# The last four of 32 inner tiles of an MLP's second product as plain block products instead of seven-product ones

## The chip, the cores and the metric

The kernel runs on one core of one Trainium2 chip. The metric is the device time of one execution in microseconds (us); the figure for a kernel is the median of its runs. Five engines work side by side in a core, each on its own list of instructions in a fixed order: TensorE (PE, matmuls), VectorE (DVE), ScalarE (ACT), GpSimd (POOL) and SyncE (SP, which here only issues DMA transfers). An engine waits where an instruction needs something that another engine or a transfer has not yet delivered, or a buffer that is not yet free. SBUF is the on-chip memory of 128 partitions, PSUM the small memory into which matmuls accumulate.

## What is computed

The reference is a decoder layer with a mixing part, cross-attention and an MLP, on 1024 tokens of width 1024 in float32. Only its end matters here:

```python
hf = rmsnorm(x, norm_mlp[l])
x = x + jnp.square(jax.nn.relu(hf @ mlp_w1[l])) @ mlp_w2[l]
...
return rmsnorm(x, norm_final)
```

The hidden width is 4096. The first product (hf with mlp_w1) gives the hidden values, which are made non-negative and squared; the second product (with mlp_w2) sums over the 4096 hidden values, that is over 32 inner tiles of 128. Its result is added to x, and every row of 1024 values is then divided by its root mean square and multiplied by a gain.

## The kernel before

**Number format.** Every float32 operand of a matmul is split into a high and a low part: ACT writes the high part (`split`, L70, a cast), and DVE or POOL subtracts it from the source to get the low part (L71). A product is then three matmuls into the same PSUM tile: high by high, high by low, low by high (`mm3`, L59, L60, L61). A matmul is 128 x 128 by 128 x 512.

**Seven products in place of eight.** Both MLP products treat their operands as 2 x 2 blocks. `LEFT` and `RIGHT` (L1058 and L1059) name for each k from 1 to 7 the block, or the sum or difference of blocks, that stands on either side. The weight's sums S1 to S4 are formed by `left` (L1064 to L1071, four instructions on tiles); those of the other side are T1 to T4.

**First product** (`mlp1`, called by `mlp_in` for pairs p = 0 to 15, seven products each). A pair yields two tiles `hab`, each with two blocks: B11 and B12, B21 and B22, made non-negative and squared on the way (`emit`, L1149 to L1155). When all four blocks of a pair are there, four subtractions on DVE (L1160 to L1163) form T1, T2, T3 and T4, and four DMA writes (L1165 to L1167) put the seven tiles of the names in `H1` (L1062) into the DRAM buffer `h1`: 512 KB each for the two `hab` and for `ht`, 256 KB for T4. Two neighbouring pairs, p = 2c and p = 2c + 1, fill `h1[c]`.

**Second product** (`mlp2`, called by `mlp_out` for passes c = 0 to 7). Pass c takes four of the 32 inner tiles. `w2_raw` loads 2 MB of weights (L1171) into one buffer of the pool `slotA` (four buffers, which the hidden units share) and calls `left` on POOL (L1066 to L1070). For each of the seven products `w2_unit` splits the weight operand (ACT L70, then L71 on POOL, in pass 7 on DVE for four of the seven) into a buffer of `wpool` (four buffers), and `h1_unit` loads the hidden operand (512 KB, L1188) through a buffer of `stage` (three buffers) and splits it (ACT L70, DVE L71). Weight loads and hidden loads are issued by SP in the program's order (`after("wdma", ...)`). Then four tiles st = 0 to 3 follow: six matmuls into one PSUM tile of the pool `m2` (six buffers), and one DVE instruction that adds the PSUM tile to the accumulator `acc[k]` for this product (`add`, L1199). So there are seven accumulators of 128 x 4 x 512 in SBUF; x itself is loaded into those of k = 2, 4, 5 and 3 in pass 0 (L1210), where the accumulators of k = 1, 6 and 7 are written by ACT.

**The last pass.** In pass 7 the seven accumulators are also put together, with `add` on tiles of 128 x 512: after a tile of product 1 comes acc[6] += acc[1] on DVE and acc[2] += acc[1] on POOL, and so on, each as soon as its product's tile is there. Four of the sums then are the four blocks of the result: acc[2] and acc[4] make one tile of rows, acc[5] and acc[3] another. Products come in the order 1, 6, 7, 2, 4, 5, 3, so the four rows of acc[2] and acc[4] are complete with product 4 and the other four with product 3. `out_rows` ends a row: for its first half a square with sum on ACT (L1242) and a product with the gain on POOL (L1243); for its second half the other square (L1249), the sum of both (POOL, L1251), the reciprocal root (`rstd`, DVE L96 and POOL L97), and then the two halves of the output, one on ACT (L1253) and one on DVE (L1255), each with a DMA to the output.

**What sets the order.** The program is written in the order above, but a scheduler orders the instructions of every engine by what they depend on and by which buffers are free. Instructions that are independent of the work around them may therefore stand earlier on an engine than in the program's text. Buffers are released tile by tile.

## Time and profile before

| | before |
|---|---|
| median of 3 runs (lowest to highest) | 2452.02 us (2450.01 to 2455.37) |
| the profiled execution's own time | 2450.84 us |
| its span, first to last instruction | 2448.9 us |
| mean granted TensorE clock | 0.985 of full speed |
| instructions | 31204 |
| shares of the chain that ended last | PE 51%, DVE 20%, DMA 11%, issue 8%, POOL 5%, ACT 4% |

The profile is of one execution. Rows of its views name an engine, a source line, the operation and the program's names for output and inputs; "x4" behind a row counts instructions that stand together, and the brackets give the idle time of the engine just before it and what ended that. Names say which buffers are meant: `wu` and `hu` are the split weight and hidden operands, `w` the loaded weights, `sth` the loaded hidden tile, `s` a sum of weight blocks, `ps` a PSUM tile, `acc` an accumulator, `xsf`, `ssf` and `rsf` the tiles of an output row, `hab` and `ht` the blocks of the first product.

### The profile page before, as it was taken

How to read it: one execution, taken by the hardware profiler on the slowest of the kernel's cores; microseconds unless marked ns; L12 is line 12 of the kernel's file. 1: busy time of each engine (PE TensorE's matmuls, PEld its weight loads, DVE VectorE, ACT ScalarE, POOL GpSimd, SP SyncE). 2: the span in 40 equal slices, each digit the busy share in tenths (PEclk: the TensorE clock that was granted, in tenths of full speed). 3: DMA queues.
4: the chain of work that ended last, by engine and by line, in shares of the span. 5: the costliest groups of instructions: out<-in, count | busy, mean ns of one | idle time of the engine just before them, and what ended most of it. 6: DMA issues, size and time to landing. Idle time of an engine off the chain costs nothing.

```text
span 2448.9 us, 31204 instructions
## 1 busy us (share of the span) xinstructions
PE 2312.1 (94%) x11132; PEld 1901.4 (78%) x11132; DVE 1885.1 (77%) x2920; ACT 1043.4 (43%) x1823; POOL 997.8 (41%) x644
## 2 busy tenths in 40 slices
PE   9999999999999989899998988999989999899996
PEld 7888878888887867677877766788768888778884
DVE  7677387877797787897787888345788888788888
ACT  5444355555555444545244444135432222343333
POOL 1122212221215434455422214034155555698787
PEclk9999999999999999999999989999999999999999
DMA  4222222222225345443576785343324443734431
GB/s 172 80 86 70 65 61 70 66 61 65 61 51 186 123 153 189 144 159 131 193 257 224 249 281 183 112 163 104 113 83 166 152 160 135 276 136 173 160 137 73
DMA packets 137258, 338.27 MB, mean 138 GB/s; under 512 B 17152, under 2 KB 27393, under 8 KB 137104
## 3 DMA queue, kind: packets, MB, share of 16 engines
q1 hardware_dynamic: 136528, 334.44, 41.5%
q8 instruction: 89, 1.46, 0.3%
q10 hardware_dynamic: 576, 1.84, 0.2%
q14 instruction: 65, 0.53, 0.1%
HBM read 229.21 MB, written 98.63 MB: 134 GB/s over the span
## 4 chain that ended last, share of the span: by engine, by line
PE 51%; DVE 20%; DMA 11%; issue 8%; POOL 5%; ACT 4%; SPq 0%; DVEq 0%; POOLq 0%; ACTq 0%
PE ps L61 7%; PE ps L59 7%; PE ps L60 7%; POOL wu L71 3%; PE psq L59 2%; PE psq L61 2%; PE psq L60 2%; PE sc L458 2%; PE psk L61 2%; DVE block L71 2%; PE psk L60 2%; PE psk L59 2%; DVE acc L1199 2%; DMA st<-oTs 1%; PE psv L60 1%
## 5 line engine op out<-in xcount | busy, mean ns | idle before, releaser
L59 PE MATMUL ps<-block,wu 128*128 128x512 f32 x1428 | 567.6, 398 | 48.3 <-DVE sf L1126 16.1
L61 PE MATMUL ps<-block,wu 128*128 128x512 f32 x1428 | 564.8, 396 | 22.3 <-DVE wu L71 15.2
L60 PE MATMUL ps<-block,wu 128*128 128x512 f32 x1428 | 560.7, 393 | 0.2 <-DVE block L71 0.2
L71 POOL TENSOR_TENSOR wu<-st,wu 128x512 fp32r<-128x512 f32 x144 | 226.0, 1577 | 385.4 <-ACT wu L70 341.8
L59 PEld LDWEIGHTS ps<-block,wu 128*128 128x128 f32 x1428 | 271.0, 190 | 111.9 <-ACT wu L70 29.0
L61 PEld LDWEIGHTS ps<-block,wu 128*128 128x128 f32 x1428 | 270.5, 189 | 90.5 <-DVE wu L71 18.6
L60 PEld LDWEIGHTS ps<-block,wu 128*128 128x128 f32 x1428 | 270.8, 190 | 60.0 <-DVE block L71 1.1
L70 ACT CAST wu<-st 128x512 fp32r<-128x512 f32 x240 | 141.3, 618 | 156.7 <-DVE st L1066 63.1
L59 PE MATMUL ps<-wu,hu 128*128 128x512 f32 x448 | 177.2, 395 | 16.9 <-DVE acc L1199 14.1
L71 POOL TENSOR_TENSOR w<-st,w 128x1024 fp32r<-128x1024 f32 x50 | 124.7, 2505 | 161.3 <-ACT w L70 161.3
L61 PE MATMUL ps<-wu,hu 128*128 128x512 f32 x448 | 174.7, 392 | 3.8 <-DVE hu L71 3.8
L60 PE MATMUL ps<-wu,hu 128*128 128x512 f32 x448 | 175.5, 392 | 0.0
L1199 DVE TENSOR_TENSOR acc<-acc,ps 128x512 f32<-128x512 f32 x216 | 137.8, 677 | 20.5 <-PE ps L61 20.0
L71 POOL TENSOR_TENSOR wu<-sf,wu 128x512 fp32r<-128x512 f32 x63 | 116.3, 1859 | 53.5 <-ACT wu L70 51.7
L71 DVE TENSOR_TENSOR hu<-sth,hu 128x1024 fp32r<-128x1024 f32 x56 | 121.1, 2167 | 20.4 <-ACT hu L70 19.9
L466 ACT ACTIVATE p<-sc,mx 128x256 f32<-128x256 f32 (+7 forms) x128 | 94.8, 741 | 69.9 <-DVE mx L463 50.2
L71 DVE TENSOR_TENSOR wu<-st,wu 128x512 fp32r<-128x512 f32 x96 | 90.1, 954 | 35.1 <-ACT wu L70 35.1
L59 PEld LDWEIGHTS ps<-wu,hu 128*128 128x128 f32 x448 | 84.6, 189 | 40.8 <-DVE acc L1199 12.2
L61 PEld LDWEIGHTS ps<-wu,hu 128*128 128x128 f32 x448 | 84.7, 189 | 22.9 <-DVE hu L71 5.1
L59 PE MATMUL psk<-block,w 128*128 128x512 f32 x256 | 102.2, 399 | 0.0
L61 PE MATMUL psk<-block,w 128*128 128x512 f32 x256 | 101.4, 396 | 0.0
L60 PE MATMUL psk<-block,w 128*128 128x512 f32 x256 | 101.3, 396 | 0.0
(389 smaller groups left out, 5638.5 us busy)
## 6 DMA issues: line engine op xcount, KB each, us to landing
sth<-h SPq DMA_DIRECT2D x56, 512.0 KB, 9.5
st<-in_w SPq DMA_DIRECT2D x32, 512.0 KB, 4.3
h<-hab SPq DMA_DIRECT2D x32, 512.0 KB, 2.8
w<-in_w SPq DMA_DIRECT2D x8, 2048.0 KB
sgb<-gsp SPq DMA_DIRECT2D x48, 256.0 KB, 4.6
gsp<-l SPq DMA_DIRECT2D x44, 256.0 KB, 4.0
acc<-y SPq DMA_DIRECT2D x40, 256.0 KB, 4.1
st<-in_w_br SPq DMA_DIRECT2D x18, 512.0 KB, 5.9
```

Of the source, the lines that this page charges most:

```text
L59: nc.tensor.matmul(ps, lhsT=lhs.hi, rhs=rhs.hi, start=start, stop=False)
L60: nc.tensor.matmul(ps, lhsT=lhs.hi, rhs=rhs.lo, start=False, stop=False)
L61: nc.tensor.matmul(ps, lhsT=lhs.lo, rhs=rhs.hi, start=False, stop=stop)
L70: ins = self.nc.scalar.copy(dst.hi, src)
L71: self.lo_ins = (lo_engine or self.nc.vector).tensor_tensor(dst.lo, src, f32(dst.hi), op=ALU.subtract)
L458: nc.tensor.matmul(sc[:, b * HB:b * HB + e], lhsT=qt[:, c, part, cols], rhs=k[b][:, c, 0:e], start=part == 0, stop=part == 1)
L466: nc.scalar.activation(p[:, 0:n], sc[:, 0:n], AF.Exp, bias=mx, accum_out=l)
L1199: eng.tensor_tensor(acc[k][:, st, :], acc[k][:, st, :], x if isinstance(x, bass.AP) else acc[x][:, st, :], op=ALU.add)
```

## The change

Pass 7 becomes a function of its own, `mlp2_last`, which computes the last four inner tiles as plain 2 x 2 block products: each of the four blocks of the result takes two products, eight in all, into the same PSUM tile (12 matmuls). No S or T is needed there, so `w2_raw` returns before `left` for c = 7, and `mlp1` ends for the last two pairs (p = 14 and 15) before the four subtractions and writes only the two `hab` tiles; `H1_LAST` names the four blocks that then lie in `h1[7]`. All eight operands, four weight blocks and four hidden blocks, are split ahead of the products; the weight blocks of the first half of the columns have their low parts on DVE, the others on POOL.

The seven accumulators are put together as they stand after pass 6: for each st seven additions on DVE (L1235). Then, for each st and each of its two rows, the two blocks of the row are computed and added to the accumulator (L1245), and the row is ended as before. A whole row is finished at a time, in eight steps.

```diff
+    H1_LAST = ("B11", "B12", "B21", "B22")
...
         if self.product(k, c, self.hf, self.p6(self.mps), v if p < 2 else nc.gpsimd, emit):
             a, b = c["h"]
+            dst = self.h1[p // 2][:, :, p % 2, :]
+            if p // 2 == 7:
+                for i, x in enumerate((a, b)):
+                    nc.sync.dma_start(dst[2 * i:2 * i + 2].rearrange("u p c -> p u c"), x)
+                return
             t, t4 = self.xw.tile([P, 2, HB], F32, tag="ts", name="ht", bufs=2), self.sraw[:, 6 + p % 2, :]
             tt(t[:, 0], a[:, 1], a[:, 0], ALU.subtract)
             tt(a[:, 1], b[:, 1], a[:, 1], ALU.subtract)
             tt(t[:, 1], b[:, 1], t[:, 0], ALU.subtract)
             tt(t4, b[:, 0], t[:, 1], ALU.subtract)
-            dst = self.h1[p // 2][:, :, p % 2, :]
             for i, x in enumerate((a, b, t)):
                 nc.sync.dma_start(dst[2 * i:2 * i + 2].rearrange("u p c -> p u c"), x)
             nc.sync.dma_start(dst[6], t4)
...
         t = self.slotA.tile([P, 4, D], F32, tag="s", name="w2")
         self.after("wdma", self.nc.sync.dma_start(t, self.a["w_2"][4 * c:4 * c + 4].rearrange("f p d -> p f d")))
         raw = {f"A{i + 1}{j + 1}": t[:, j::2, i * HB:(i + 1) * HB] for i in range(2) for j in range(2)}
+        if c == 7:
+            return raw
         self.left(raw, *(self.xw.tile([P, 2, HB], F32, tag=t, name="s2", bufs=2) for t in ("xt", "xt", "ts")), self.nc.gpsimd)
         return raw
...
         t = self.utile[:, self.n_units % 2]
         self.n_units += 1
         st = self.stage.tile([P, 2, HB], F32, tag="st", name="sth")
-        self.after("wdma", self.nc.sync.dma_start(st, self.h1[c, self.H1.index(name)]))
+        self.after("wdma", self.nc.sync.dma_start(st, self.h1[c, (self.H1_LAST if c == 7 else self.H1).index(name)]))
         u = Split(t[:, 0], t[:, 1])
         self.split(u, st)
         return u
-    def mlp2(self, c, acc, mps, gf):
+    def mlp2(self, c, acc, mps):
         nc, v, g = self.nc, self.nc.vector, self.nc.gpsimd
-        first, last = c == 0, c == 7
-        def add(k, x, st, eng=v):
-            eng.tensor_tensor(acc[k][:, st, :], acc[k][:, st, :], x if isinstance(x, bass.AP) else acc[x][:, st, :], op=ALU.add)
+        first = c == 0
         raw = self.w2_raw(c)
-        if last:
-            for st in range(4):
-                add(3, 5, st, g)
         for k in (1, 2, 4, 5, 7, 6, 3) if first else (1, 6, 7, 2, 4, 5, 3):
-            w, h = self.w2_unit(raw[self.LEFT[k]], v if last and k in (7, 4, 5, 3) else g), self.h1_unit(c, self.RIGHT[k])
+            w, h = self.w2_unit(raw[self.LEFT[k]], g), self.h1_unit(c, self.RIGHT[k])
             if first and k in (2, 4, 5):
                 x3 = self.x3.rearrange("(t s p) c -> s p t c", s=2, p=P)
                 for i, s, d in {2: ((2, 0, 0),), 4: ((4, 0, 1),), 5: ((5, 1, 1), (3, 1, 0))}[k]:
...
                 if first and k in (1, 6, 7):
                     nc.scalar.copy(acc[k][:, st, :], ps)
                 else:
-                    add(k, ps, st)
-                if not last:
-                    continue
-                if k == 1:
-                    add(6, 1, st)
-                    add(2, 1, st, g)
-                elif k == 6:
-                    add(7, 6, st)
-                    add(3, 6, st, g)
-                elif k == 7:
-                    add(4, 7, st)
-                    add(5, 7, st, g)
-                elif k == 5:
-                    add(3, ps, st)
-                self.out_rows(st, k, acc[k][:, st, :], gf)
...
+                    v.tensor_tensor(acc[k][:, st, :], acc[k][:, st, :], ps, op=ALU.add)
+    def mlp2_last(self, acc, mps, gf):
+        nc, v = self.nc, self.nc.vector
+        raw = self.w2_raw(7)
+        w, h = {}, {}
+        for k in range(2):
+            for x in ("A1", "A2"):
+                w[f"{x}{k + 1}"] = self.w2_unit(raw[f"{x}{k + 1}"], v if x == "A1" else nc.gpsimd)
+            h[f"B{k + 1}1"] = self.h1_unit(7, f"B{k + 1}1")
+        for k in range(2):
+            h[f"B{k + 1}2"] = self.h1_unit(7, f"B{k + 1}2")
+        for st in range(4):
+            for o, x in ((2, 1), (6, 1), (7, 6), (4, 7), (3, 6), (3, 5), (5, 7)):
+                v.tensor_tensor(acc[o][:, st, :], acc[o][:, st, :], acc[x][:, st, :], op=ALU.add)
+            for j in range(2):
+                xs = self.xw.tile([P, D], F32, tag=("ts", "xs")[j], name="xsf", bufs=2)
+                ss = self.small.tile([P, 2], F32, tag="ssf", name="ssf", bufs=8)
+                row = (2 * st + j + 4) % 8 * P
+                for i in range(2):
+                    ps = mps.tile([P, HB], F32, tag="m2", name="ps2")
+                    self.mmk(ps, [(h[f"B{k + 1}{j + 1}"][:, r, st * P:(st + 1) * P], w[f"A{i + 1}{k + 1}"][:, r, :])
+                                  for k in range(2) for r in range(2)])
+                    x = acc[2 + 2 * i + j][:, st, :]
+                    v.tensor_tensor(x, x, ps, op=ALU.add)
+                    sl = slice(i * HB, (i + 1) * HB)
+                    nc.scalar.activation(xs[:, sl], x, AF.Square, accum_out=ss[:, i:i + 1])
+                    if i == 0:
+                        nc.gpsimd.tensor_tensor(xs[:, sl], x, gf[:, sl], op=ALU.mult)
+                rs = self.small.tile([P, 1], F32, tag="rs", name="rsf", bufs=4)
+                nc.gpsimd.tensor_tensor(rs, ss[:, 0:1], ss[:, 1:2], op=ALU.add)
+                self.rstd(rs, rs, 1.0 / D, 1e-6)
+                nc.scalar.activation(xs[:, 0:HB], xs[:, 0:HB], AF.Copy, scale=rs)
+                nc.sync.dma_start(self.out[row:row + P, 0:HB], xs[:, 0:HB])
+                v.scalar_tensor_tensor(xs[:, HB:], x, rs, gf[:, HB:], op0=ALU.mult, op1=ALU.mult)
+                nc.sync.dma_start(self.out[row:row + P, HB:], xs[:, HB:])
...
             for i, k in enumerate(ks):
                 acc[k] = t[:, i]
         gf = self.gain(self.xw, 4)
-        for c in range(8):
-            self.mlp2(c, acc, mps, gf)
+        for c in range(7):
+            self.mlp2(c, acc, mps)
+        self.mlp2_last(acc, mps, gf)
     def run(self):
```

What takes the place of `out_rows` (L1235 to L1256 before, deleted) is in the last lines of `mlp2_last`; its steps on ACT, POOL and DVE are the same.

Three places show how instructions move in the lists of the engines.

The first is DVE in pass 6 and 7. Of the change, these rows stand where pass 6's products 6 and 7 are added up (`acc_18412` is the buffer of the accumulators k = 1 and 2, `acc_18414` that of 7 and 6; `ps2` is a PSUM tile, `hu` a split hidden operand):

```order
L1219 TENSOR_TENSOR acc_18414<-acc_18414,ps2_20192 128x512
L1235 TENSOR_TENSOR acc_18414<-acc_18414,acc_18412 128x512
L1219 TENSOR_TENSOR acc_18414<-acc_18414,ps2_20200 128x512
L71 TENSOR_TENSOR hu_20385<-sth_20386,hu_20385 128x1024
L1219 TENSOR_TENSOR acc_18414<-acc_18414,ps2_20208 128x512
L1235 TENSOR_TENSOR acc_18414<-acc_18414,acc_18412 128x512
L1219 TENSOR_TENSOR acc_18414<-acc_18414,ps2_20216 128x512
L1235 TENSOR_TENSOR acc_18414<-acc_18414,acc_18412 128x512
```

Before, DVE's additions of one accumulator to another begin behind pass 6, between the PSUM additions of pass 7's first product:

```order
L1199 TENSOR_TENSOR acc_18426<-acc_18426,ps2_20456 128x512
L1199 TENSOR_TENSOR acc_18428<-acc_18428,acc_18426 128x512
L1199 TENSOR_TENSOR acc_18426<-acc_18426,ps2_20466 128x512
L1199 TENSOR_TENSOR acc_18428<-acc_18428,acc_18426 128x512
L1199 TENSOR_TENSOR acc_18426<-acc_18426,ps2_20476 128x512
```

So the additions between accumulators have moved ahead, as soon as the tile that they need has its last product of pass 6; 10 of the 28 stand up to the end of pass 6's fourth product.

The second is DVE at the end. Of the change, these rows end the fifth and the sixth of the eight output rows (`rsf` is the row's reciprocal root, `xsf` its output):

```order
L1245 TENSOR_TENSOR acc_18412<-acc_18412,ps2_20641 128x512
L1245 TENSOR_TENSOR acc_18413<-acc_18413,ps2_20657 128x512
L96 TENSOR_SCALAR rsf_20672<-rsf_20672 128x1
L1255 SCALAR_TENSOR_TENSOR xsf_20639<-acc_18413,rsf_20672,gain_18416 128x512
L1245 TENSOR_TENSOR acc_18415<-acc_18415,ps2_20682 128x512
L1245 TENSOR_TENSOR acc_18413<-acc_18413,ps2_20698 128x512
L96 TENSOR_SCALAR rsf_20713<-rsf_20713 128x1
L1255 SCALAR_TENSOR_TENSOR xsf_20680<-acc_18413,rsf_20713,gain_18416 128x512
```

Before, the additions of the last product and the ends of its four rows stand like this:

```order
L1199 TENSOR_TENSOR acc_18429<-acc_18429,ps2_20823 128x512
L96 TENSOR_SCALAR rsf_20798<-rsf_20798 128x1
L1199 TENSOR_TENSOR acc_18429<-acc_18429,ps2_20840 128x512
L1255 SCALAR_TENSOR_TENSOR xsf_20739<-acc_18429,rsf_20798,gain_18430 128x512
L96 TENSOR_SCALAR rsf_20815<-rsf_20815 128x1
L96 TENSOR_SCALAR rsf_20832<-rsf_20832 128x1
L1255 SCALAR_TENSOR_TENSOR xsf_20752<-acc_18429,rsf_20815,gain_18430 128x512
```

Before, the additions of all four rows stand ahead of the first L1255. In the change the L1255 of a row stands ahead of both additions of the next one, so each row's chain through ACT and POOL comes back to DVE before DVE goes on.

The third is SP at the seam between the two products of the MLP. Before, these rows stand around pass 0's weight load (`hab_18234`, `hab_18182`, `ht_18273` and `sraw_15893` are pair 14's writes, `x3` is x for the accumulators):

```order
L1166 DMA h1_85<-hab_18234 128x2x512
L1171 DMA w2_18432<-in_w_2 128x4x1024
L1166 DMA h1_85<-hab_18182 128x2x512
L1166 DMA h1_85<-ht_18273 128x2x512
L1167 DMA h1_85<-sraw_15893 128x512
L1188 DMA sth_18445<-h1_85 128x1024
L1188 DMA sth_18484<-h1_85 128x1024
L1210 DMA acc_18426<-x3_87 128x4x512
L1166 DMA h1_85<-hab_18374 128x2x512
```

With the change:

```order
L1163 DMA h1_85<-hab_18234 128x2x512
L1210 DMA acc_18412<-x3_87 128x4x512
L1163 DMA h1_85<-hab_18182 128x2x512
L1176 DMA w2_18418<-in_w_2 128x4x1024
L1195 DMA sth_18431<-h1_85 128x1024
L1195 DMA sth_18470<-h1_85 128x1024
L1195 DMA sth_18511<-h1_85 128x1024
L1195 DMA sth_18551<-h1_85 128x1024
L1163 DMA h1_85<-hab_18367 128x2x512
```

Pair 14's last two writes are gone, a load of x stands ahead of the weight load instead of behind the second hidden load, and four hidden loads instead of two stand ahead of pair 15's first write. Pass 1's weight load comes, in both, behind the seventh hidden load.

21 lines of the change are left out of this document (removed).

## The prediction

> **What bounds the kernel now.** I read the page's first part and the windows of the last hundred microseconds, then the rows of each engine there. Columns of a window: its length, then busy time of PE, weight loads, DVE, ACT and POOL, the granted clock, the DMA share and GB/s.
>
> ```profile
> PE 2312.1 (94%) x11132; PEld 1901.4 (78%) x11132; DVE 1885.1 (77%) x2920; ACT 1043.4 (43%) x1823; POOL 997.8 (41%) x644
> 2350.00:2400.00 50.00, 48.16 (x213) 39.55 (x213) 43.82 (x47) 17.16 (x17) 41.95 (x18) 1.00 0.32 116
> 2400.00:2449.00 49.00, 27.25 (x108) 19.36 (x108) 42.64 (x55) 17.41 (x41) 32.33 (x34) 0.90 0.23 86
> ```
>
> TensorE (PE) bounds the program as a whole, but not its end: in the last 49 us it works 27 us and DVE 43. The change acts there. Rows below are start, duration, engine, line, operands, and in brackets the idle time before them with what ended it; the last row is a wait: total, times, longest.
>
> ```profile
> 2384.52 1.05 ACT L70 CAST wu<-w 128x1024 fp32r<-128x1024 f32 x1 [2.49 <-PE ps L61]
> 2404.59 0.47 PE L59 MATMUL ps<-wu,hu 128*128 128x512 f32 x1 [1.68 <-DVE acc L1199]
> 2405.36 0.39 PE L59 MATMUL ps<-wu,hu 128*128 128x512 f32 x1
> 2406.72 0.39 PE L59 MATMUL ps<-wu,hu 128*128 128x512 f32 x1
> 2436.34 0.39 PE L61 MATMUL ps<-wu,hu 128*128 128x512 f32 x1
> PE ps L59 <- DVE acc L1199: 10.4, 8, 1.8
> ```
>
> The ACT cast waits for the weight buffer that the last matmul of pass 6 (c = 6) gives back, so pass 7 starts on PE at about 2384.5. Six matmuls take 1.36 us (2405.36 to 2406.72), 0.2267 each. Pass 7 has 7 products x 4 row tiles x 6 = 168 matmuls, 38.1 us when dense; its last one ends at 2436.7, after 52.2 us. So 14.1 us of it is waiting, mostly for DVE to empty PSUM (10.4 us). What DVE does there, by groups over 2380 to 2449 (count, busy us, mean ns, idle):
>
> ```profile
> L1199 POOL TENSOR_TENSOR acc<-acc 128x512 f32<-128x512 f32 x16 | 26.7, 1700 | 2.5 <-DVE acc L1199 2.5
> L1199 DVE TENSOR_TENSOR acc<-acc,ps 128x512 f32<-128x512 f32 x36 | 23.1, 675 | 0.0
> L1199 DVE TENSOR_TENSOR acc<-acc 128x512 f32<-128x512 f32 x12 | 20.0, 1690 | 0.1
> 2439.35 0.69 DVE L1199 TENSOR_TENSOR acc<-acc,ps 128x512 f32<-128x512 f32 x1
> 2443.89 0.75 DVE L1255 SCALAR_TENSOR_TENSOR xsf<-acc,rsf,gain 128x512 f32<-128x512 f32 x1 [0.66 <-POOL rsf L97]
> ```
>
> An add from PSUM costs 0.68 us, an add of two SBUF tiles 1.69 us beside POOL's own adds. After PE's end four output rows still queue up: the last accumulation starts at 2439.35, the last L1255 at 2443.89, and from there to the span's end (2448.9) it is 5.0 us.
>
> **The change, part by part.** *Matmuls.* Pass 7 gets 16 groups of 12 matmuls: 192 x 0.2267 = 43.5 us, 5.4 more. One output row (two groups) takes PE 5.44 us.
>
> *DVE's adds.* Counts are even: before 32 from PSUM and 12 between tiles on DVE, 16 on POOL; after, 16 and 28, all on DVE. In the order after, 10 of the 28 stand among pass 6's adds up to its fourth product, 3 among its sixth, 15 behind pass 6. What such an add costs without POOL is seen where the first product ends; what it meets in pass 6 are POOL's weight splits.
>
> ```profile
> 2112.62 2.79 DVE L1147 TENSOR_TENSOR ht<-hab 128x512 f32<-128x512 f32 x1
> 2115.44 0.69 DVE L1147 TENSOR_TENSOR hab<-hab 128x512 f32<-128x512 f32 x1
> 2347.75 0.69 DVE L1199 TENSOR_TENSOR acc<-acc,ps 128x512 f32<-128x512 f32 x1 [0.46 <-PE ps L61]
> 2348.48 3.35 DVE L71 TENSOR_TENSOR hu<-sth,hu 128x1024 fp32r<-128x1024 f32 x1
> 2358.46 2.44 POOL L71 TENSOR_TENSOR wu<-s,wu 128x1024 fp32r<-128x1024 f32 x1 [2.63 <-ACT wu L70]
> 2363.90 2.43 POOL L71 TENSOR_TENSOR wu<-s,wu 128x1024 fp32r<-128x1024 f32 x1 [3.00 <-ACT wu L70]
> 2376.38 2.47 DVE L1199 TENSOR_TENSOR acc<-acc,ps 128x512 f32<-128x512 f32 x4
> 2380.23 1.96 DVE L71 TENSOR_TENSOR wu<-w,wu 128x1024 fp32r<-128x1024 f32 x1 [0.51 <-ACT wu L70]
> 2419.76 1.21 DVE L71 TENSOR_TENSOR hu<-sth,hu 128x1024 fp32r<-128x1024 f32 x1
> ```
>
> So an add of two tiles lies between 0.69 (free) and 1.69 (the mean beside POOL). POOL splits some 2.4 us in every 5.4 us of pass 6, and after it only two weight tiles and eight products with the gain are left to it. I take 0.65 a piece in sequence (their ends overlap a little), plus 1.0 for the six or so of 28 that meet POOL: 18.2 + 6 = 24.2 us. Both ends are kept: 28 x 0.65 = 18.2 and 28 x 1.69 = 47.3.
>
> The Trainium skill, "SBUF — State Buffer", section "Who interferes with whom", says that a DVE instruction with two SBUF inputs and a GpSimd instruction that reads SBUF exclude each other for a whole instruction. The trace agrees (0.69 against 1.69 and 2.79). By that rule, POOL's 16 adds were no help to DVE, and half a split (1.2) instead of 1.0 for each meeting would add 1.2 us to the sum.
>
> DVE's account from pass 6's first add (2347.75) to the third output row: 28 + 4 adds from PSUM at 0.62 (2.47 for four), 19.8; seven splits of the transposed hidden tiles, one at 3.35, five at 1.2, one at 1.7, together 11.1; two weight splits at 1.96, 3.9; the 28 adds, 24.2; two L1255 and their waits, 2.7. That is 61.7 us: 2409.4.
>
> *The eight rows.* Each ends in the same steps; here they are in the trace before.
>
> ```profile
> 2416.84 0.68 DVE L1199 TENSOR_TENSOR acc<-acc,ps 128x512 f32<-128x512 f32 x1
> 2417.55 0.64 ACT L1242 ACTIVATE xsf<-acc 128x512 f32<-128x512 f32 x1 [13.55 <-DVE acc L1199]
> 2418.35 1.45 POOL L1243 TENSOR_TENSOR xsf<-acc,gain 128x512 f32<-128x512 f32 x1 [1.98 <-ACT xsf L1242]
> 2420.90 1.27 DVE L1199 TENSOR_TENSOR acc<-acc,ps 128x512 f32<-128x512 f32 x2
> 2422.20 0.63 ACT L1249 ACTIVATE xsf<-acc 128x512 f32<-128x512 f32 x1 [2.20 <-DVE acc L1199]
> 2423.01 0.35 POOL L1251 TENSOR_TENSOR rsf<-ssf 128x1 f32<-128x1 f32 x1 [0.87 <-ACT xsf L1249]
> 2424.21 1.77 DVE L1255 SCALAR_TENSOR_TENSOR xsf<-acc,rsf,gain 128x512 f32<-128x512 f32 x1
> ```
>
> If both halves of a row are ready, POOL's product with the gain starts 1.5 us after the first add (2416.84 to 2418.35) and takes 1.45; then L1251, and L1255 1.2 us after that (2423.01 to 2424.21): 4.2 us. DVE stands in line for it, so the next row's add comes 0.7 later: 4.9 us a row. With the third row at 2409.4, the eighth starts at 2409.4 + 5 x 4.9 = 2433.9 and its L1255 at 2438.1; with the 5.0 of the tail the span ends at 2443.1.
>
> PE must not be later. The second weight block A12 is split on DVE behind 24 PSUM adds (14.9), six hidden splits (9.4), A11's split (2.0), 13 tile adds (8.5 + 4) and its own 1.9: 2388.4. PE has used up its first six matmuls at 2385.9, so it waits 2.5 and ends at 2384.5 + 2.5 + 43.5 = 2430.5. From PE's end an unhurried row needs 0.2, then 2.7 from its second add (2421.5, the second of the pair at 2420.90) to L1255, then 5.0: 2438.4. DVE is later, by 4.7. **This part gains 2448.9 - 2443.1 = 5.8 us.**
> DVE may lag PE by at most six PSUM groups, 6.8 us. At its worst, the fourth product of pass 6, it starts the first add at 2347.75 + 12 x 0.62 + 5.8 (three splits) + 8 x 0.65 + 4 = 2370.2, ended 2370.8; PE finished that group 15 groups before 2384.5, at 2364.1, so the limit is 2370.9. I cost PE's wait here at nothing, but the cover is 0.1 us thick: what DVE loses more up to there, PE loses too.
>
> *The seam between the two products.* The last two pairs lose eight subtractions on DVE and four writes of 1.5 MB in all. On SP an accumulator's load of 1 MB now stands ahead of pass 0's weight load, and the hidden loads ahead of the last pair's write.
>
> ```profile
> 2087.02 0.37 SPq L1171 DMA_DIRECT2D w<-in_w  x1
> 2110.47 0.79 PE L59 MATMUL ps<-wu,hu 128*128 128x512 f32 x1 [2.71 <-DVE hab L1147]
> 2127.55 0.39 SPq L1171 DMA_DIRECT2D w<-in_w  x1
> 2139.34 2.86 POOL L1066 TENSOR_TENSOR s<-w 128x1024 f32<-128x1024 f32 x1 [7.53 <-DMA w<-in_w]
> 2169.02 0.47 PE L59 MATMUL ps<-wu,hu 128*128 128x512 f32 x1 [0.86 <-DVE acc L1199]
> 2177.49 1.22 DVE L71 TENSOR_TENSOR hu<-sth,hu 128x1024 fp32r<-128x1024 f32 x1 [5.03 <-ACT hu L70]
> 2179.37 0.50 PE L59 MATMUL ps<-wu,hu 128*128 128x512 f32 x1 [0.58 <-DVE acc L1199]
> 2182.80 0.47 PE L59 MATMUL ps<-wu,hu 128*128 128x512 f32 x1 [1.77 <-DVE acc L1199]
> ```
>
> Pass 1's weight load goes out at 2127.55, behind hidden loads that wait for DVE's splits; POOL waits 7.5 us for it, and what follows, DVE's 5 us for a hidden tile and PE's three waits (0.86 + 0.58 + 1.77 = 3.2), is late for the same reason. In the order after, the two splits that those loads wait for stand ahead of pass 0's adds, not among them, so the load needs only the end of pass 0's second product, some 4 us earlier by my estimate (42 matmuls from 2110.47, a dozen of them at half pace). I credit the 3.2 and 0.8 more for smaller waits before them. Against it, DVE's last add of the first product moves behind a second split: 0.5 later than 2110.47. Net gain 3.5; bounds 5 gained (all of DVE's wait) and 2 lost (if the 1 MB ahead of the first load delays everything by its share of the 9 us that 2 MB take).
>
> **Sum.** 5.8 + 3.5 = 9.3 us off a span of 2448.9, 2439.6; the profiled execution took 2450.84, 1.94 more, hence 2441.5. The median of the runs, 2452.02, is 1.2 above that execution; on its scale the change gives 2442.7.
>
> **The rivals.** *DVE catches up.* If rows cost DVE less than 4.9, or few adds meet POOL, PE's end counts: 2438.4, 4.7 better, 2438. For it: every add is then free of POOL after pass 6. Against it: five rows recover only 5 x 0.54 = 2.7 of the lag.
>
> *The seam gives nothing.* The loads are bound by bytes, not by when they are issued, and DVE's waits move with them: 2452.0 - 5.8 = 2446.2, or 2448 with the 2 us lost. For it: POOL's wait is for a transfer. Against it: it was issued late.
>
> *PE waits in pass 6 instead.* The ten early adds push DVE past the six buffers; three more meetings with POOL there, 3 us, and a slower A12 split (2 us) reach PE directly, and with a seam that gives nothing, 2452.0 - 0.8 = 2451.2.
>
> *The adds keep their price (slower).* Place: the 28 adds on DVE. If each costs 1.69, as beside POOL, the account grows by 47.3 - 24.2 = 23.1 us, and nothing behind hides it, since DVE sets the end: 2442.7 + 23.1 = 2465.8. It decides from 9.3/28 = 0.33 above my mean of 0.86 on, at 1.2 us an add. For it: the adds of two tiles in pass 7 before all cost that. Against it: there POOL had 16 of its own beside them, 26.7 us, which are gone.
>
> *It doesn't do what it says:* excluded by the order, where the 16 groups of 12 stand.
>
> **How the numbers follow.** The forecast, 2438.5 to 2446, has 0.46; DVE catching up 0.20; the seam giving nothing 0.14; PE waiting in pass 6 0.12; the adds' price 0.08. About 0.2% (4.9 us, 2447.1 and 2456.9) is what a measurement of this kernel can tell from no change. Faster by more: 0.46 + 0.20 + two fifths of the seam's case, 0.06, 0.72. Within: the other 0.08 and the 0.12, 0.20. Slower: 0.08. The range is 2434 (both the first rival and the seam's upper bound) to 2450, which leaves out the last rival and part of the one before it.
>
> **What would show it.** Right: DVE's L1235 at 0.7 to 0.9 on average; pass 7 on PE with one wait of 1 to 4 us at its start and then dense, some 46 us; rows 4.9 to 5.5 apart at L1255, DVE idle in each for L97; no PE waits near 2170 to 2183. Wrong: L1235 above 1.2; PE waiting for DVE inside pass 6; a first product's end followed by a PE gap longer than the two of before.

## The result, and the profile after

The changed kernel takes 2438.6 us (median of 12 runs, 2433.31 to 2449.82) against 2452.09 us for the kernel before in the same series (12 runs, 2447.76 to 2457.38). The ratio is 0.9942, with a 95% interval of 0.9931 to 0.9954: 11 to 17 us faster. 2442.7 had been forecast, with a range of 2434 to 2450. The profiled execution took 2435.75 us, its span is 2434.0 us (2448.9 before).

The first line of the page and the windows of the end (columns as in the prediction):

```profile
PE 2321.0 (95%) x11156; PEld 1914.3 (79%) x11156; DVE 1867.4 (77%) x2907; ACT 1036.6 (43%) x1817; POOL 950.6 (39%) x623
2350.00:2400.00 50.00, 49.89 (x220) 40.96 (x219) 49.42 (x65) 14.07 (x18) 17.67 (x9) 1.00 0.25 95
2400.00:2434.00 34.00, 25.10 (x111) 20.46 (x109) 15.23 (x29) 13.82 (x33) 13.00 (x20) 0.91 0.29 108
```

Before, DVE was the busy engine of the end and PE waited; now PE is dense to 2425 and DVE is busy for less than half of the last 34 us. To see where the time went, the span is cut at two places: at the start of the last matmul of the first product (2103.13 before), and at ACT's weight cast that waits for pass 6's last matmul (2384.52 before). Between them lies S, behind the second T. These are the rows of the changed kernel:

```profile
2101.71 0.39 PE L61 MATMUL ps<-block,wu 128*128 128x512 f32 x1
2102.62 0.47 PE L59 MATMUL ps<-wu,hu 128*128 128x512 f32 x1 [0.52 <-ACT hu L70]
2106.90 0.76 PE L60 MATMUL ps<-wu,hu 128*128 128x512 f32 x1 [3.81 <-POOL wu L71]
2107.46 0.63 PE L61 MATMUL ps<-wu,hu 128*128 128x512 f32 x1
2152.31 0.79 PE L59 MATMUL ps<-wu,hu 128*128 128x512 f32 x1 [2.94 <-DVE acc L1219]
2381.27 1.06 ACT L70 CAST wu<-w 128x1024 fp32r<-128x1024 f32 x1 [3.46 <-PE ps L61]
2424.71 0.39 PE L61 MATMUL ps<-wu,hu 128*128 128x512 f32 x1
```

S went from 281.4 to 279.6, T from 64.4 to 52.7. The other 1.4 us of the span's 14.9 lie ahead of the first cut, where the code is the same; that cut lies anywhere from 2096.8 to 2107.5 in the executions below, so it is left out of the account. In T, PE's part, up to the start of its last matmul, fell from 51.8 to 43.4 (192 dense matmuls in place of 168 with 14 us of waits), and what is left from there to the end from 12.6 to 9.3.

What DVE does within T, by groups, first before and then after (count, busy us, mean ns, idle ahead):

```profile
L1199 DVE TENSOR_TENSOR acc<-acc,ps 128x512 f32<-128x512 f32 x34 | 21.8, 675 | 0.0
L1199 DVE TENSOR_TENSOR acc<-acc 128x512 f32<-128x512 f32 x12 | 20.0, 1690 | 0.1
L1255 DVE SCALAR_TENSOR_TENSOR xsf<-acc,rsf,gain 128x512 f32<-128x512 f32 x8 | 8.0, 1006 | 1.8 <-POOL rsf L97 1.5
L71 DVE TENSOR_TENSOR hu<-sth,hu 128x1024 fp32r<-128x1024 f32 x4 | 6.9, 1723 | 0.0
L71 DVE TENSOR_TENSOR wu<-s,wu 128x1024 fp32r<-128x1024 f32 x2 | 2.4, 1211 | 0.0
```
```profile
L1235 DVE TENSOR_TENSOR acc<-acc 128x512 f32<-128x512 f32 x16 | 11.9, 782 | 0.0
L1245 DVE TENSOR_TENSOR acc<-acc,ps 128x512 f32<-128x512 f32 x16 | 10.4, 679 | 0.0
L1255 DVE SCALAR_TENSOR_TENSOR xsf<-acc,rsf,gain 128x512 f32<-128x512 f32 x8 | 6.0, 751 | 5.1 <-POOL rsf L97 5.1
L1219 DVE TENSOR_TENSOR acc<-acc,ps 128x512 f32<-128x512 f32 x5 | 3.2, 674 | 0.0
L71 DVE TENSOR_TENSOR hu<-sth,hu 128x1024 fp32r<-128x1024 f32 x1 | 2.2, 2220 | 0.0
```

With two small ones the groups add up to 62 us before and 36 after. They overlap a little: DVE is busy for 58.0 of T's 64.4 us before and for 33.5 of 52.7 after. Three things each take some 8 us off DVE's work in T: 13 PSUM additions fewer behind the cut, 12 of the 28 tile additions done ahead of it, and fewer splits behind it.

### The profile page after: what moved, and what is told of

Same layout as the page of the kernel before. It is cut to its first block, busy times and chain, and to the rows that moved or that the text cites. A ratio compares the mean times of both kernels' runs of the same rounds, so it can differ in the third digit from the quotient of the medians.

```text
span 2434.0 us, 31149 instructions
## 1 busy us (share of the span) xinstructions
PE 2321.0 (95%) x11156; PEld 1914.3 (79%) x11156; DVE 1867.4 (77%) x2907; ACT 1036.6 (43%) x1817; POOL 950.6 (39%) x623
## 4 chain that ended last, share of the span: by engine, by line
PE 56%; DVE 19%; DMA 8%; issue 8%; POOL 6%; ACT 3%; SPq 0%; POOLq 0%; DVEq 0%; ACTq 0%
PE ps L59 8%; PE ps L61 8%; PE ps L60 8%; POOL wu L71 3%; PE psq L59 2%; PE psq L61 2%; PE psq L60 2%; PE sc L458 2%; PE psk L61 2%; PE psk L60 2%; PE psk L59 2%; DVE block L71 2%; DMA st<-oTs 2%; PE psv L59 1%; PE psv L61 1%
## 5 line engine op out<-in xcount | busy, mean ns | idle before, releaser
L59 PE MATMUL ps<-block,wu 128*128 128x512 f32 x1428 | 570.7, 400 | 40.3 <-DVE sf L1127 17.7
L60 PE MATMUL ps<-wu,hu 128*128 128x512 f32 x456 | 179.5, 394 | 3.9 <-POOL wu L71 3.8
L59 PE MATMUL ps<-wu,hu 128*128 128x512 f32 x456 | 179.4, 393 | 3.5 <-DVE acc L1219 2.9
L61 PE MATMUL ps<-wu,hu 128*128 128x512 f32 x456 | 179.1, 393 | 0.0
L71 POOL TENSOR_TENSOR wu<-sf,wu 128x512 fp32r<-128x512 f32 x63 | 116.0, 1855 | 49.4 <-ACT wu L70 47.8
L1219 DVE TENSOR_TENSOR acc<-acc,ps 128x512 f32<-128x512 f32 x184 | 117.6, 677 | 18.0 <-PE ps L61 17.9
```

Source lines behind the costliest of these rows:

```text
L59: nc.tensor.matmul(ps, lhsT=lhs.hi, rhs=rhs.hi, start=start, stop=False)
L60: nc.tensor.matmul(ps, lhsT=lhs.hi, rhs=rhs.lo, start=False, stop=False)
L61: nc.tensor.matmul(ps, lhsT=lhs.lo, rhs=rhs.hi, start=False, stop=stop)
L71: self.lo_ins = (lo_engine or self.nc.vector).tensor_tensor(dst.lo, src, f32(dst.hi), op=ALU.subtract)
L1219: v.tensor_tensor(acc[k][:, st, :], acc[k][:, st, :], ps, op=ALU.add)
```

## The experiments

All are compared with the kernel before, in series of their own, so the ratios can be set side by side but the medians of different series cannot (before: 2452.1, 2447.8, 2448.4 and 2448.7 us in the four series). S and T are from one profiled execution each.

| kernel | S | T | median, us | ratio to before (95%) |
|---|---|---|---|---|
| before | 281.4 | 64.4 | | |
| the change | 279.6 | 52.7 | 2438.6 | 0.9942 (0.9931 to 0.9954) |
| 1: seam's subtractions kept | 283.3 | 53.0 | 2440.4 | 0.9968 (0.9954 to 0.9981) |
| 2: before, all additions on DVE | 281.4 | 68.1 | 2452.5 | 1.0022 (1.0010 to 1.0034) |
| 3: 16 additions on POOL | 277.5 | 65.1 | 2447.8 | 0.9999 (0.9987 to 1.0010) |
| 4: additions behind pass 6 | 279.8 | 54.0 | 2434.8 | 0.9947 (0.9932 to 0.9963) |
| 5: rows ended on DVE | 281.6 | 52.0 | 2436.8 | 0.9952 (0.9940 to 0.9964) |
| 6: A11, A12 split first | 281.8 | 52.6 | 2437.7 | 0.9957 (0.9943 to 0.9971) |
| 7: as 3, behind the splits | 278.2 | 61.0 | 2441.0 | 0.9968 (0.9956 to 0.9981) |
| 8: groups of 6 matmuls | 282.1 | 54.9 | 2438.7 | 0.9965 (0.9953 to 0.9977) |
| 9: 4 and 8 together | 278.1 | 58.3 | 2439.5 | 0.9961 (0.9947 to 0.9974) |
| 10: rows overlapped on DVE | 281.6 | 50.8 | 2434.0 | 0.9938 (0.9922 to 0.9953) |
| 11: 6, and DVE's order at the seam | 278.9 | 52.7 | 2433.7 | 0.9937 (0.9923 to 0.9952) |
| 12: 10 and 11 together | 280.0 | 50.8 | 2433.4 | 0.9945 (0.9929 to 0.9960) |

T repeats well: the four executions whose pass 7 is that of the change have 52.6 to 53.0. S does not: the eight with the change's code at the seam (the change, 3 to 5 and 7 to 10) lie between 277.5 and 282.1. PE's matmuls come in the same order in all these kernels, so S can be cut further by counting them from the first cut. Up to the 200th matmul the eight take 55.5 to 58.0 us (before: 55.6). From there to the 1008th, the last of pass 5, they take 183.2 to 183.9 (before: 187.3). Pass 6 then takes 38.6 to 38.8 us, but 40.3 to 40.4 in kernels 5, 8 and 10 (before: 38.6). The second and the third difference are explained below, with kernel 1 and under "The thin cover in pass 6"; why the first part varies by 2.5 is left open.

**1. The seam's work kept.** In `mlp1` the early return goes; the second subtraction's target is free, so that B12 stays:

```diff
-            if p // 2 == 7:
...
-                return
-            tt(a[:, 1], b[:, 1], a[:, 1], ALU.subtract)
+            tt(t4 if p // 2 == 7 else a[:, 1], b[:, 1], a[:, 1], ALU.subtract)
```

> The changed kernel, but the last two pairs of the first product keep their four subtractions each and the writes of T1, T2, T3 and T4 (into rows of the buffer that nothing reads). Two stages: S, from the last matmul of the first product to pass 7's first weight cast that waits for pass 6's last matmul (281.4 us before, 279.6 with the change), and T, from there to the span's end (64.4 and 52.7). Theory: DVE's eight subtractions and 1.5 MB of writes are what S gained; S returns to 281 to 282, T stays at 52.7 +- 0.5, the time is 2440.4. Rival: the 1.8 of S is the order of the loads or varies from run to run; S stays within 0.5 of 279.6 and the time at 2438.6.

S came out at 283.3, above both, T at 53.0, so the tail does not depend on the subtractions and writes. In S they bring three waits of PE in pass 1 back, nearly as long as before (0.86, 0.58 and 1.77):

```profile
2162.89 0.47 PE L59 MATMUL ps<-wu,hu 128*128 128x512 f32 x1 [0.88 <-DVE acc L1215]
2173.17 0.50 PE L59 MATMUL ps<-wu,hu 128*128 128x512 f32 x1 [0.49 <-DVE acc L1215]
2176.59 0.47 PE L59 MATMUL ps<-wu,hu 128*128 128x512 f32 x1 [1.77 <-DVE acc L1215]
```

The part from the 200th to the 1008th matmul, which holds them, takes 187.2 us, as before (187.3), against 183.2 to 183.9 in the eight: taking the subtractions and writes out, with the order of the loads that comes with it, is worth 4 us there. That S is above 282 has another reason: this kernel also has the wait in pass 6, which makes that pass 1.8 longer.

**2. The old pass 7 with all additions on DVE.** At the four places of this kind:

```diff
-                    add(2, 1, st, g)
+                    add(2, 1, st)
```

> The kernel before, with POOL's 16 additions between accumulators in pass 7 moved to DVE; nothing else. Theory (DVE's 1.69 us per addition was waiting for POOL's own, so POOL's 16 were no relief): DVE's additions of two tiles fall to 0.65 to 0.9 each, 28 of them cost 18 to 24 us in place of 12 at 20.0, so DVE's account changes by -2 to +4 and T stays at 62 to 68 (64.4 before); time 2450 to 2456. The gain then comes from the plain products and from additions that moved into pass 6. Rival: POOL's additions alone made the end long; T falls to 53 to 56 and the time to 2441 to 2444.

T rose to 68.1, at the upper edge of the theory's range. The group of tile additions on DVE within T, PE's longest wait, and the split that it is for, first here and then in the kernel before:

```profile
L1199 DVE TENSOR_TENSOR acc<-acc 128x512 f32<-128x512 f32 x28 | 20.8, 795 | 0.0
2434.32 1.22 PE L60 MATMUL ps<-wu,hu 128*128 128x512 f32 x2 [5.48 <-DVE wu L71]
2433.05 1.22 DVE L71 TENSOR_TENSOR wu<-s,wu 128x1024 fp32r<-128x1024 f32 x1
```
```profile
2422.10 1.21 DVE L71 TENSOR_TENSOR wu<-s,wu 128x1024 fp32r<-128x1024 f32 x1
```

28 additions take DVE 20.8 us where 12 took 20.0 beside POOL's 16: what POOL did, DVE paid for in waiting, to within a microsecond. This shows the step of the prediction that rested on the rows 0.69 and 1.69. But giving POOL's work back won nothing by itself. The scheduler also moved something else: DVE's last weight split now stands behind the ends of the first four output rows (their L1255 start at 2422.35 to 2431.78), where before it stood ahead of them, and PE waits 5.5 us for it. So the rise of T is not the price of the additions. The rival (T 53 to 56) falls all the same: DVE is busy for 55.8 us of this T, and 3.6 more pass from the end of its last instruction to the span's end.

**3 and 7. The change with 16 additions on POOL.** In 7 POOL's additions are also ordered behind its last weight split.

```diff
-                v.tensor_tensor(acc[o][:, st, :], acc[o][:, st, :], acc[x][:, st, :], op=ALU.add)
+                e = nc.gpsimd if (o, x) in ((2, 1), (3, 6), (3, 5), (5, 7)) else v
+                e.tensor_tensor(acc[o][:, st, :], acc[o][:, st, :], acc[x][:, st, :], op=ALU.add)
```

> The changed kernel, but four of the seven additions for each tile (16 in all, the same ones as before the change) on POOL. Theory: POOL and DVE exclude each other there; DVE's 12 remaining additions cost 1.2 to 1.7 each and its hidden splits more, and POOL's 16 need 27 us; T rises from 52.7 to 60 or more, time 2446 to 2455. Rival: POOL takes 14 us of additions off DVE and DVE was what set the end; T 50 to 52.5, time 2436 to 2438.5.

> As the kernel with 16 of the additions on POOL (T 65.1, of which 11.4 were PE waiting for a weight split that stood behind 12 of them on POOL), but here POOL's additions all stand behind its two weight splits. Theory: what made that kernel slow was the place of the split; POOL's 16 additions (24.4 us) then lie beside DVE's 12, which cost about 1.2 each, and beside the rows; T 53 to 58, with POOL late for the first rows. Rival: POOL's additions stop DVE so much that DVE's third row starts 10 us later; T 60 or more. If T is under 52 the additions on POOL would be a relief after all.

Both are slower, by 12.4 and 8.3 us in T. Kernel 3 lies in its theory's range and kernel 7, with 61.0, in its rival's, but neither for the reason expected. Kernel 3, POOL's queue and the PE row that waits for it:

```profile
2385.17 11.39 POOL L1236 TENSOR_TENSOR acc<-acc 128x512 f32<-128x512 f32 x8 [4.76 <-DVE acc L1219]
2396.52 2.34 POOL L71 TENSOR_TENSOR wu<-w,wu 128x1024 fp32r<-128x1024 f32 x1
2398.91 0.79 PE L60 MATMUL ps<-wu,hu 128*128 128x512 f32 x1 [11.35 <-POOL wu L71]
```

The split of a weight block stands behind eight additions. In kernel 7 it does not, and the first row's L1257 (the sum of squares, L1251 in the change) is what queues there:

```profile
2393.09 6.28 POOL L1237 TENSOR_TENSOR acc<-acc 128x512 f32<-128x512 f32 x5
2399.33 0.19 POOL L1257 TENSOR_TENSOR rsf<-ssf 128x1 f32<-128x1 f32 x1
2399.56 0.15 DVE L96 TENSOR_SCALAR rsf<-rsf 128x1 f32<-128x1 f32 x1 [12.62 <-POOL rsf L1257]
```

DVE stands idle for 12.6 us because the short instruction it needs waits in POOL's line.

**4. All additions behind pass 6.** Each addition between accumulators is ordered behind DVE's last PSUM addition of pass 6 (`sum_ins`):

```diff
-                v.tensor_tensor(acc[o][:, st, :], acc[o][:, st, :], acc[x][:, st, :], op=ALU.add)
+                ins = v.tensor_tensor(acc[o][:, st, :], acc[o][:, st, :], acc[x][:, st, :], op=ALU.add)
+                self.tc.add_manual_dep(ins.ins, self.sum_ins.ins.name, ...)
```

> The changed kernel, but all 28 additions between accumulators stand on DVE behind the last addition of pass 6 (13 of them stood among pass 6's). Theory: the 13 (11 us at 0.87) filled gaps of DVE in pass 6 for the most part; behind pass 6 they are in line, DVE's third row starts 5 to 10 us later, the eight rows of 4.5 us against PE's 5.44 recover up to 4.7 of it, and T becomes 54 to 60, with PE waiting for DVE in pass 7. Time 2440 to 2446. Rival: PE's dense matmuls alone set the end and DVE has room; T within 0.7 of 52.7.

T rose by only 1.3, the lower end of what the theory allowed, and its steps failed: PE waits nowhere in pass 7, and no row is 5 us late. The first additions of the fifth and of the eighth row:

```profile
2411.10 0.68 DVE L1248 TENSOR_TENSOR acc<-acc,ps 128x512 f32<-128x512 f32 x1
2424.66 1.28 DVE L1248 TENSOR_TENSOR acc<-acc,ps 128x512 f32<-128x512 f32 x2
```

With the cut at 2378.81 the fifth row starts 32.3 us behind it (31.0 in the change), the eighth 45.8 (44.6). The additions of later tiles slip in between the first rows, where DVE would wait for ACT and POOL: its waits ahead of L96 and L1255 fall from 15.6 us to 10.9. PE does not notice the lag; that this is because six PSUM tiles now hold 6 x 2.72 = 16.3 us of its work is argued from the count; kernel 9, whose six tiles hold half of that, does have a wait.

**8 and 9. Groups of 6, alone and with late additions.** Each block is computed in two PSUM tiles:

```diff
-                    ps = mps.tile([P, HB], F32, tag="m2", name="ps2")
...
+                    for k in range(2):
+                        ps = mps.tile([P, HB], F32, tag="m2", name="ps2")
+                        self.mmk(ps, [(h[f"B{k + 1}{j + 1}"][:, r, st * P:(st + 1) * P], w[f"A{i + 1}{k + 1}"][:, r, :])
+                                      for r in range(2)])
+                        v.tensor_tensor(x, x, ps, op=ALU.add)
```

> The changed kernel, but each block of the result takes its two products in two PSUM tiles of 6 matmuls, with two DVE additions, in place of one tile of 12: 32 PSUM additions in pass 7 (as before the change) in place of 16; PE's work is the same. Theory: that pass 7 runs dense on PE rests on the halved number of PSUM additions and on six buffers that last for 16 us in place of 8; with 32 of them DVE has 9.6 us more to do ahead of the end, PE waits for DVE again, T 56 to 62, time 2442 to 2448. Rival: the early additions between accumulators and the order by rows alone give the gain; DVE waits 15 us in its rows anyway and takes the 16 additions in there; T within 1.5 of 52.7.

> Both of two earlier kernels at once: all 28 additions between accumulators behind pass 6 (alone T 54.0), and pass 7 in 32 groups of 6 matmuls with 32 PSUM additions (alone T 54.9). DVE's additions in pass 7 are then those of the kernel before with all of them on DVE (T 68.1). Theory: the two costs add, 52.7 + 1.3 + 2.2 = 56.2, T 55.5 to 58; the other 10 us or so come from operands: four weight and four hidden blocks, split ahead of everything, where seven of each were split in between. Rival: one of the two gave DVE the room that the other needed; without both T goes to 61 to 66, and the early additions and the groups of 12 are the gain after all.

Kernel 8 has T 54.9, between the two ranges: the 16 extra additions cost 2.2, since most fit into DVE's waits ahead of L96 and of the rows' last products, which fall from 15.6 us to 7.5. With both, T is 58.3, 2 more than the sum and just above the theory's range, and PE waits once for a microsecond or more:

```profile
2410.55 0.50 PE L59 MATMUL ps<-wu,hu 128*128 128x512 f32 x1 [2.07 <-DVE acc L1249]
```

So T can be walked down in steps: 64.4 before; 68.1 with POOL's additions on DVE; 58.3 with plain blocks, the same 28 and 32 additions and all of them late; 52.7 with groups of 12 and early additions. The second step, 9.8, is the largest. In it DVE's groups within T keep their additions (28 at 20.8 us and 21.6), but the splits are gone: 9.8 us of hidden and weight splits in kernel 2, none in kernel 9, where eight operands are ready ahead of the cut. But DVE's busy time falls by less, from 55.8 to 50.2, and kernel 2 holds PE's wait of 5.5 for a split that had moved. That step also changes the products and the order by rows, so that the splits make it is argued from the groups, not shown by a run of their own.

**5 and 10. The rows' ends.** In 5 both halves of a row are ended by DVE; in 10 nothing changes but that a row's L96 is ordered behind the next row's first PSUM addition and its L1255 behind the second. The edit of 5:

```diff
-                        nc.gpsimd.tensor_tensor(xs[:, sl], x, gf[:, sl], op=ALU.mult)
+                        x0 = x
...
-                nc.scalar.activation(xs[:, 0:HB], xs[:, 0:HB], AF.Copy, scale=rs)
+                v.scalar_tensor_tensor(xs[:, 0:HB], x0, rs, gf[:, 0:HB], op0=ALU.mult, op1=ALU.mult)
```

> The changed kernel, but both halves of an output row are finished on DVE (two instructions of the kind L1255 in place of POOL's product with the gain, ACT's scaling and one L1255). T, from pass 7's first weight cast that waits for pass 6's last matmul to the span's end, was 52.7. Theory: DVE has nearly caught up with PE by the last row, so the end is PE's end and one row's chain; that chain loses POOL's product ahead of L1251 (1.26) and DVE's remaining lag (1.3) and gets 0.67 for the second product; rows come at PE's pace of 5.44 at the end, T 50.3 to 51.5, time 2436.5 to 2437.5. Rival: the rows of 4.5 on DVE still set the end; eight shorter rows take 4 us or more off, T under 49.5. Rival 2: the end is the output transfer; T within 0.5 of 52.7.

> The changed kernel, but on DVE a row's L96 stands behind the first PSUM addition of the next row and its L1255 behind the second, so that a row's way through ACT and POOL no longer holds DVE up; no work is added or removed. Theory: DVE catches up with PE in pass 7 and the last row starts at PE's last matmul (it came 1.3 later); T = 43.4 + 0.4 + 7.0 = 50.8 (50.3 to 51.3), time 2436.7. Rival: the last row's chain is as long or longer because the row before it stands in it; T 52.2 or more.

Kernel 5 missed: T 52.0, rows 4.5 apart. The first of the two products starts 3.2 behind the row's first addition, 0.6 sooner than L1255 in the change, and the second one takes that back; the 0.7 that T lost lie behind the start of the last L1255 (3.65 in place of 4.32). Some 0.4 of it is the last output transfer, which SP issues 0.77 behind that start; in the change it is 1.17, since both halves are ready at once there and SP issues the other one first. Kernel 10 has T 50.8, as forecast; its last row on DVE:

```profile
2426.62 0.69 DVE L1251 TENSOR_TENSOR acc<-acc,ps 128x512 f32<-128x512 f32 x1 [1.97 <-PE ps L61]
2428.43 0.15 DVE L1262 TENSOR_SCALAR rsf<-rsf 128x1 f32<-128x1 f32 x1 [0.46 <-POOL rsf L1259]
2429.25 0.75 DVE L1270 SCALAR_TENSOR_TENSOR xsf<-acc,rsf,gain 128x512 f32<-128x512 f32 x1 [0.67 <-POOL rsf L1265]
```

DVE waits for PE (1.97), not PE's result for DVE: the last addition starts 0.43 behind PE's last matmul (2426.19).

**6, 11 and 12. The seam.** In 6 POOL splits A11 and A12 at pass 0 ahead of its first and second sum; in 11, in addition, DVE's last addition of the first product (`hab_ins`) stands ahead of all hidden splits but the first; 12 joins 10 and 11. The core of the edits, in `w2_raw` (6) and `h1_unit` (11):

```diff
+        for k in (1, 2) if c == 0 else ():
+            self.w_first[k] = self.w2_unit(raw[f"A1{k}"], self.nc.gpsimd)
+            lo.append(self.lo_ins)
         self.left(raw, ...)
+        for x, y in zip(self.left_ins, lo):
+            self.tc.add_manual_dep(x.ins, y.ins.name, ...)
...
+        if c == 0 and name != self.RIGHT[1]:
+            self.tc.add_manual_dep(self.lo_ins.ins, self.hab_ins.ins.name, ...)
```

> The changed kernel, but at pass 0 POOL splits the weight blocks A11 and A12 ahead of the first and of the second sum of weight blocks, as before the change; nothing else moves on any engine. Theory: PE's wait of 3.8 at the first product's end is for A11's low part, which stood behind two sums (2.95 + 3.24); it falls to 1 to 2, and S (279.6; 277.5 to 279.8 in three runs with the same seam) to 275.5 to 278. Rival: DVE's split of the hidden tiles (one ends at 2101.9, the next at 2107.9) is as late, the wait only changes its name, S 277.5 to 280.

> The kernel with A11 and A12 split ahead of POOL's sums at pass 0, and in addition DVE's last addition of the first product stands ahead of the second hidden split instead of behind it (that split took 3.4 and PE waited 4.4 for a PSUM buffer). Theory: POOL and DVE each held PE, one behind the other; with both moved PE's waits between the first product's end and 2112 fall from 5.2 (0.5 + 3.8 in the changed kernel) to under 2.5, and S from 281.8 to 277 to 279. Rival: the splits that were moved back come late for the next product, and the wait goes there; S stays at 280 or more.

> The row order on DVE of the kernel with overlapped rows and the seam's order of the kernel before this one, together. Theory: T 50.3 to 51.3 and S as there (277 to 279), they do not touch each other; time about 4 us under the changed kernel's 2438.6. Rival: what one gains at the seam the fourth product of pass 6 takes back in PE waits (1.0 in four of the kernels so far); S 280 or more, time 2436 to 2437.

In 6 the wait for POOL (3.81) became one for DVE, as the rival said; S, at 281.8, is above both ranges, 1.8 of it from the wait in pass 6. Behind a hidden split that took 3.37 beside POOL's sum stands the addition that frees the PSUM tile:

```profile
2107.30 3.37 DVE L71 TENSOR_TENSOR hu<-sth,hu 128x1024 fp32r<-128x1024 f32 x1
2110.59 0.68 DVE L1149 TENSOR_TENSOR hab<-ps,ut 128x512 f32<-128x512 f32 x1
2111.32 0.79 PE L59 MATMUL ps<-wu,hu 128*128 128x512 f32 x1 [4.36 <-DVE hab L1149]
```

In 11 both are moved, and PE's waits up to 2112 are two of 1.0 and 1.1; S fell to 278.9, inside the theory's range, but also inside that of the change itself. Part of the wait had moved on:

```profile
2104.47 0.50 PE L59 MATMUL ps<-wu,hu 128*128 128x512 f32 x1 [1.08 <-DVE hab L1149]
2120.62 0.79 PE L59 MATMUL ps<-wu,hu 128*128 128x512 f32 x1 [3.61 <-DVE acc L1232]
```

Up to the 200th matmul kernels 11 and 12 take 54.8 and 54.4 us, less than any of the eight, so these orders probably did shorten the seam; in both, the wait in pass 6 takes 1.8 back, and in 12 three waits in pass 1 (0.5, 0.3 and 1.7) take more. Kernel 12 kept T 50.8 and missed its theory with S 280.0, the rival's value. The intervals of 10, 11, 12 and the change overlap, so none is shown to be faster than the change by the clock; that T is 1.9 shorter in 10 and 12 is shown by the traces.

## Why the prediction was right, and where it was off

**The end.** That the change acts in T, that PE becomes dense there and that 16 groups of 12 are cheaper for DVE was right; the size was half: 5.8 forecast, 11.7 measured. Counted from the cut, the prediction had the third row at 24.9, the eighth at 49.4 and the end at 58.6. The trace has 22.1, 44.6 and 52.7:

```profile
2403.34 1.28 DVE L1245 TENSOR_TENSOR acc<-acc,ps 128x512 f32<-128x512 f32 x2
2406.32 0.15 DVE L96 TENSOR_SCALAR rsf<-rsf 128x1 f32<-128x1 f32 x1 [1.71 <-POOL rsf L1251]
2407.81 1.28 DVE L1245 TENSOR_TENSOR acc<-acc,ps 128x512 f32<-128x512 f32 x2
2425.86 1.28 DVE L1245 TENSOR_TENSOR acc<-acc,ps 128x512 f32<-128x512 f32 x2
2429.68 0.75 DVE L1255 SCALAR_TENSOR_TENSOR xsf<-acc,rsf,gain 128x512 f32<-128x512 f32 x1 [0.66 <-POOL rsf L97]
```

Four terms were mis-sized, all in the same direction. DVE's account to the third row was 2.8 too high, with two weight splits at 1.21 in place of 1.96 and tile additions that come every 0.60 where nothing meets them, not 0.65. A row takes 4.5 (2403.34 to 2425.86 for five), not 4.9: its price had been read from a row of the kernel before whose steps met others' work. From the eighth row's first addition to L1255 it is 3.8, not 4.2, and from there to the end 4.3, not 5.0. These are 2.8 + 2.0 + 0.4 + 0.7 = 5.9, the whole difference in T. What came about is nearly the first rival, DVE catching up, which had 2438 and a chance of 0.20: rows recover 0.94 each on PE, not 0.54. Kernel 10 gives the rest of DVE's lag, at most 1.9 us. The wait of 2.5 for A12 was 0.3. So two of the signs named for the forecast did not appear: a PE wait of 1 to 4 us at the start of pass 7, and rows 4.9 to 5.5 apart.

**The price of an addition** (0.7 to 0.9 expected) is 0.87 as a mean of the 28, so the slower rival falls; kernel 2 shows the mechanism behind it. POOL's 16 were no help to DVE. The prediction had drawn this from the rule that the Trainium skill, "SBUF — State Buffer", states in the section "Who interferes with whom", and the two groups (12 at 20.0, 28 at 20.8) agree.

**The thin cover in pass 6.** PE's wait there was costed at nothing, with 0.1 us of cover. It did not hold: of the eight kernels that have ten tile additions on DVE up to the fourth product, seven show a PE wait of 1.0 us there, and only the execution of the change itself does not; those with later or fewer additions on DVE (3, 4, 7, 9) have none. Which it is depends on two splits that start within half a microsecond. The change, then kernel 5:

```profile
2371.19 1.22 DVE L71 TENSOR_TENSOR wu<-w,wu 128x1024 fp32r<-128x1024 f32 x1
2371.51 3.16 POOL L71 TENSOR_TENSOR wu<-w,wu 128x1024 fp32r<-128x1024 f32 x1 [8.29 <-ACT wu L70]
```
```profile
2371.67 2.40 POOL L71 TENSOR_TENSOR wu<-w,wu 128x1024 fp32r<-128x1024 f32 x1 [8.63 <-ACT wu L70]
2372.21 2.95 DVE L71 TENSOR_TENSOR wu<-w,wu 128x1024 fp32r<-128x1024 f32 x1
2375.81 0.50 PE L59 MATMUL ps<-wu,hu 128*128 128x512 f32 x1 [1.04 <-DVE acc L1219]
```

The split that starts first takes 1.22 on DVE or 2.40 on POOL, the other one 3.16 or 2.95. When POOL is first, which it is in all seven, DVE's additions behind it are late; PE waits 1.04 here, with two shorter stops ahead of it, and pass 6 takes 40.3 us in place of 38.6. The rival that PE waits in pass 6 thus has its mechanism, at 1.8 us and not at the 5 that it counted. The change itself has a trace of one execution out of 12; which order the others had is not shown.

**The seam.** 3.5 was forecast; S fell by 1.8 in this execution and by 1.6 on the mean of the eight executions with this seam (279.8). Counted by matmuls, the 1.8 are 4.1 gained behind the 200th and 2.2 lost ahead of it. The gain is what had been credited, 3.2 and 0.8: the three waits near 2169 to 2183 are gone, and kernel 1 brings them back. The failed step is the 0.5 set against it; 2.2 stand in its place. Pass 0's last matmul still comes 3.6 us sooner behind the cut than before, although PE waits 3.81 for A11's low part behind two sums on POOL, where there were two waits of 2.6 and 2.7; the prediction had looked at SP's and DVE's order there, not at POOL's, and this wait was one of its signs of being wrong. Then PE waits 2.94 at 2152 for an addition that stands on DVE behind two hidden splits, and this wait and the slow matmuls behind it take back 5.7:

```profile
2145.03 6.63 DVE L71 TENSOR_TENSOR hu<-sth,hu 128x1024 fp32r<-128x1024 f32 x2 [4.80 <-ACT hu L70]
2151.58 1.27 DVE L1219 TENSOR_TENSOR acc<-acc,ps 128x512 f32<-128x512 f32 x2
```

**The sum.** 11.7 and 1.6 make 13.3, and the medians differ by 13.5. Two errors, 5.9 too little at the end and 1.9 too much at the seam, partly covered each other.

## What to carry to other kernels

Before moving work in a tail, add up each engine's groups from the last point at which it was hidden: here DVE was busy for 58 us of 64. Work taken out of that stretch counts only until PE is the bound: 24.5 us less on DVE gave 11.7. Do not offload two-tile additions from DVE to POOL without measuring: beside POOL's 16, DVE's 12 took as long as all 28 did on DVE alone, and short instructions that others wait for queue behind POOL's. A price for a step should come from a place where nothing meets it, with the meetings counted apart.

## What the runs showed of the hardware that was not expected

A wait of PE can cost more than its length. Behind the 3.81 us at 2106.90 the matmuls start 0.43 apart up to 2110.0 (the row of 0.63 above), behind the 2.94 at 2152.31 up to 2158.0, where they come every 0.23 otherwise; the second wait thus cost 2.9 + 14 x 0.2 = 5.7 us. The profile shows why: the granted clock is 0.50 from 2107.0 to 2110.4 and from 2151.3 to 2158.1, in the second case from 1 us before the wait ends. In the kernel before, a wait of 2.59 was followed by matmuls at 0.23 to 0.33 with a granted clock of 1.00, and the next, of 2.71 four microseconds later, by the slow ones, with a clock of 0.50 from 2108.5 to 2115.3.
